# A two-layer decoder trunk: six of eight attention-branch gates by seven products, and values and gates kept by head pairs

## The chip, the cores and the metric

The kernel runs on one core of one Trainium2 chip, in one launch. The metric is the device time of that launch in microseconds (us), as the median of several runs. A profile is one more execution, recorded by the hardware profiler, with a time of its own. Engines are named as the profile names them: PE is the matrix engine (TensorE) and PEld its loading of weights, DVE is VectorE, ACT is ScalarE, POOL is GpSimd, SP is SyncE, which here only issues transfers.

## The reference

All data is float32: 512 tokens (S), width 1024 (D), two layers. Each layer is a feed-forward part, a mixer, and a second feed-forward part, each with a norm before and after. The change is in the mixer alone:

```python
for l in range(DEPTH):                                  # DEPTH = 2
    ...
    h = rms_norm(x, gn[2])
    proj = h @ w_in[l]
    hq, hf, hi, hg, aq, ak, av, gate_a, gate_b = jnp.split(proj, IN_SPLITS, axis=-1)
    y_hg = hgrn2_mixer(hq, hf, hi, hg, lb_all[l], hgrn_head_gain[l]) @ w_branch_hgrn[l]
    y_at = swa_sink_attention(aq, ak, av, attn_sinks[l]) @ w_branch_attn[l]
    mixed = jax.nn.sigmoid(gate_a) * y_hg + jax.nn.sigmoid(gate_b) * y_at
    x = x + rms_norm(mixed @ w_out[l], gn[3])
    ...
```

`hgrn2_mixer` is a gated linear recurrence over four heads of 128, from which come the values `hi` and a gate `hg` on the output; `swa_sink_attention` is attention over a window of 128 tokens, eight heads of 64, in four blocks of 128 queries, with one more logit per head (the sink) in the denominator. `gate_a` and `gate_b`, 1024 wide each, gate the two branches that are added.

## The kernel before

**Numbers in halves.** Each float32 operand is split into a high part that PE takes in its faster format, and the low part that is left (`split`: ACT writes the high part, DVE subtracts). A product of two tiles of 128 x 128 by 512 columns is three matmuls, high by high, low by high, high by low (line 116). Line 126 is a transpose through PE.

**Weights** come from memory through `Stream`, `ws` in the code, in units of 128 x 1024 in the order of their use: SP issues the load (`w<-wall`), ACT casts the high part (line 359), DVE subtracts the low one (line 363); for some kinds of unit the low part is instead ACT's negated copy (line 355), to which a transfer issued by POOL adds the weights (line 358). The stream splits at least three units ahead of PE, has four buffers for raw units and six for each part of split ones.

**Seven products for eight.** `sevenths` makes two output tiles at once from seven products of 256 columns (an algorithm of Strassen's kind), each four blocks deep, where two plain tiles take eight blocks of 512 columns each. Its weights are four units of a pair: the first is plain, the second and third are sums of the pair's two raw units, which DVE makes (lines 341 to 345) in buffers of the tag `tt`, the fourth is a plain half. Behind the products DVE puts the two tiles together (lines 1063 to 1070). A matmul of 144 columns, `lead`, goes ahead of a pair. The moving operands are also sums, of quarters of the mixer's input, made once per layer (`pre.sums`, four calls) and kept.

**The tag `tt` has two buffers**, and the recurrence draws from it as well, once per head and level:

```python
self.t13 = sb.tile([P, D], F32, tag="tt", name=nm("tt"), bufs=2)                 # Stream, a pair's second unit
self.t = t = sb.tile([P, D], F32, tag="tt", name=nm("tt"), bufs=2)               # and its third
self.mv = mv = sb.tile([P, 2 * TT, 96], F32, tag="tt", name=nm("mv"), bufs=2)    # recurrence, before a level
```

**What sets the order.** PE runs in the order in which the code issues its work. Side work, which is the recurrence and the attention, is written as coroutines (`order.spawn`), each of which names a time in `WAIT` until its next step is due; between two blocks of weights the code runs the steps that are due by its own clock of PE's work. On the other engines a scheduler sets the order when the kernel is built. An engine then works through its list in that order.

**The mixer** runs in this order: the projections of recurrence heads 0 and 1 (`quad`, by seven products), keys, queries and values of the attention, four token tiles of recurrence values (`vs`), four of output gates (`gs`), the projections of heads 2 and 3, eight tiles of the attention branch, each a gate by a plain product (`project`) and four blocks of the branch's own weights (`branch`, `LATE = 8` of them), four pairs of tiles of the recurrence branch with their gates by seven products (`branches(recurred)`), and the output product (`down`). The four attention blocks (`attend`: scores on PE, the mask and the maximum on DVE, lines 1357 to 1368, the exponentials on ACT, line 1374, transposes of the shares on PE, copies of those on ACT, line 1396, and their product with the values) run between the projections of values, gates and heads 2 and 3; the attention branch needs all four (`attended`). The recurrence of heads 2 and 3 (per level `mv` on ACT and DVE, line 1188, products on PE, then `place`, line 1164, `queries` and `keys`, lines 1172 to 1179, on DVE) runs between the eight tiles of the attention branch; the recurrence branch needs it (`recurred`). Tanh and gating of `gs` are lines 1428 and 1429, those of a branch tile line 1444 on DVE.

PSUM has eight banks: five of the tag `acc`, in which the projections collect, and three of the tag `aux`, for everything else. Names in the profile such as `s`, `acc`, `aux`, `tt`, `whi`, `wlo` are these tags and tiles.

Of the kernel before, what the change touches and what calls it, by code (L numbers as in the profile page):

```python
# [7 lines left out]
F32 = mybir.dt.float32  # L8
F32R = mybir.dt.float32r
# [24 lines left out]
    head=2600.0, level=5000.0, last=3400.0, chunks=2600.0, states=2600.0, norm=2370.0, gate=8000.0,  # L34
    values=1200.0, scores=2000.0, exp=9000.0, shares=6000.0, turn=1900.0, turned=3000.0, rest=1200.0, lent=4200.0, apart=4000.0, block=2000.0, pair=4000.0, att0=1260.0, att1=12300.0,
)
W32, WS, AHEAD, TAIL, FIRST, EARLY, LATE = 4, 6, 3, 4, 7, 4, 8
TURN = 0
SEVEN = 16
ASIDE = 16  # L40
# [6 lines left out]
def trunk(ctx: ExitStack, tc: tile.TileContext, xin, wall, gains, lbT, hgain, sinks, c_dist, c_mask, c_ident, out):  # L47
# [16 lines left out]
    def big(dt=F32, shape=None):  # L64
        return sb.tile(shape or [P, S], dt, tag="s", name=nm("s"), bufs=SLOTS)
# [4 lines left out]
    def acc():  # L70
        return ps.tile([P, S], F32, tag="acc", name=nm("acc"), bufs=5)

    def aux():
        return ps.tile([P, S], F32, tag="aux", name=nm("aux"), bufs=3)
# [350 lines left out]
    def cut(pair, c):  # L425
        return pair[0][:, c], pair[1][:, c]
# [73 lines left out]
    def pair_split(v, how=split):  # L500
        return how(v, to=(big(F32R, [P, 2, S // 2]), big(F32R, [P, 2, S // 2])))
# [77 lines left out]
    class Pre(Quarters):  # L579


        def __init__(self, l, n):
            self.l, self.n = l, n
            self.h = []
            self.have = [0, 0]
            self.rb = None
            self.xn = {}
            self.x56, self.x37 = [], []

        def sums(self):  # L590
            k = len(self.x56)
            a = []
            for hi, lo in (self.h[k], self.h[k + 4]):
                f = big()
                nc.vector.tensor_tensor(f, hi.bitcast(F32), lo.bitcast(F32), op=ALU.add)
                a.append([f[:, c] for c in HALF])
            for x, v in zip((self.x56, self.x37), quarter_sums(a[0][0], a[1][0], a[0][1], a[1][1])):
                x.append(pair_split(v))

        def raw(self, half, i):  # L600
            return [cut(self.h[k + 4 * i], HALF[half]) for k in range(4)]
# [431 lines left out]

        mm(o[:, :n], st, mv[:, :n], True, True)

    def sevenths(pre, between=lambda: None, first=True):

        def product(o, it, c, n):  # L1040
            x = pre.operand(n)
            for k in range(4):
                wmm(o, ws.block(it, c + k), x[k], k == 0, k == 3)

        p1, p26, p57, p43 = acc()[:, :H2], acc(), acc(), aux()
        s, v = big()[:, :H2], big(F32, [P, 2, H2])
        w = ws.whole()
        if first:
            lead(p1, w.hi[:, :P], pre.operand(1)[0][0], LEAD)
        product(p1, w, 0, 1)  # L1050
        ws.hold(nc.scalar.copy(s, p1))
        product(p26[:, :H2], w, 4, 2)
        between()
        w = ws.whole()
        product(p57[:, :H2], w, 0, 5)
        product(p57[:, H2:], w, 4, 7)
        c = ws.whole()
        product(p26[:, H2:], c, 0, 6)
        ws.product()
        m = sb.tile([P, 4, H2], F32, tag="m", name=nm("m"), bufs=1)  # L1060
        pairs = [p.rearrange("p (i t) -> p i t", i=2) for p in (p26, p57, p43)]

        ws.hold(nc.vector.tensor_tensor(m[:, 0:4:2, :], pairs[0], s.unsqueeze(1).to_broadcast([P, 2, H2]), op=ALU.add))

        ws.hold(nc.vector.tensor_tensor(v, pairs[1], m[:, 2:3, :].to_broadcast([P, 2, H2]), op=ALU.add))
        product(p43[:, :H2], c, 4, 4)
        product(p43[:, H2:], ws.whole(), 4, 3)

        ws.hold(nc.vector.tensor_tensor(m[:, 3, :], p57[:, :H2], v[:, 1, :], op=ALU.add))
        ws.hold(nc.vector.tensor_tensor(m[:, 1:3, :], pairs[2], v[:, ::-1, :], op=ALU.add))  # L1070
        return m
# [178 lines left out]
    def chunk_states(hs, vs, i):  # L1250

        pu = [aux() for _ in hs]
        for n, (h, p) in enumerate(zip(hs, pu)):
            d = slice((i + n) * P, (i + n + 1) * P)
            for c in range(TT - 1):
                mm(p[:, c * P : (c + 1) * P], h.kt[:, c * P : (c + 1) * P], vs[c][:, d], True, True)
        for h, p in zip(hs, pu):
            h.st = big()
            nc.scalar.copy(h.st[:, :P], p[:, :P])
        for c in (1, 2):  # L1260
            for h, p in zip(hs, pu):
                o, u = (h.st[:, (c - x) * P : (c - x + 1) * P] for x in (0, 1))
                nc.vector.scalar_tensor_tensor(o, u, h.prod[:, c : c + 1], p[:, c * P : (c + 1) * P], op0=ALU.mult, op1=ALU.add)
        yield WAIT["states"]

    def mixer(l, pre, nxt):
        vs, gs = [], []
        oa = [None] * H

        def head(ph, pq, i):  # L1270
            f, k, q, th = big(), big(), big(), big()
# [8 lines left out]
        def outputs(i, h):  # L1280
            po = aux()
            for t in range(TT):
                c = slice(t * P, (t + 1) * P)
                mm(po[:, c], h.sd[:, t, :], vs[t][:, i * P : (i + 1) * P], True, t == 0)
                if t:
                    mm(po[:, c], h.qa[:, c], h.st[:, (t - 1) * P : t * P], False, True)
            pov = po.rearrange("p (t d) -> p t d", t=TT)
            sq = big()
            nc.scalar.activation(out=sq, in_=po, func=AF.Square)
            ss = small([P, TT], "ss")  # L1290
            nc.vector.tensor_reduce(ss, sq.rearrange("p (t d) -> p t d", t=TT), axis=AX.X, op=ALU.add)
            nc.scalar.activation(out=ss, in_=ss, func=AF.Sqrt, bias=eps_t, scale=1.0 / P)
            nc.vector.reciprocal(ss, ss)
            o = big(F32, [P, TT, P])
            nc.vector.tensor_tensor(o, pov, ss.unsqueeze(2).to_broadcast([P, TT, P]), op=ALU.mult)
            yield WAIT["norm"]
            while len(gs) < TT:
                yield 500.0
            for t in range(TT):
                nc.vector.tensor_tensor(o[:, t, :], o[:, t, :], gs[t][:, i * P : (i + 1) * P], op=ALU.mult)  # L1300
            yield WAIT["gate"]
            pt = aux()
            for t in range(TT):
                transpose(pt[:, t * P : (t + 1) * P], o[:, t, :])
            oa[i] = split(pt)

        def run(i, heads):
            yield WAIT["head"]
            box = []
            yield from recurrence_scores(heads, box)  # L1310
            if len(vs) < TT:
                while len(vs) < TT:
                    yield 500.0
                yield WAIT["lent"]
            yield from chunk_states(box, vs, i)
            for n in range(2):
                order.spawn(outputs(i + n, box[n]), n * WAIT["apart"])
# [101 lines left out]
        order.spawn(attention((1, 3)), WAIT["att1"])  # L1419


        for i, p in enumerate(project_tok(pre)):
            v = big()
            (nc.vector.tensor_copy if i % 2 else nc.scalar.copy)(v, p)
            vs.append(v)
        for p in project_tok(pre):
            g = big()
            nc.scalar.activation(out=g, in_=p, func=AF.Tanh, scale=0.5)
            nc.vector.scalar_tensor_tensor(g, g, 1.0, p, op0=ALU.add, op1=ALU.mult)
            gv = g.rearrange("p (i d) -> p i d", i=H)  # L1430
            nc.vector.tensor_tensor(gv, gv, hgh[:, l : l + 1, :].to_broadcast([P, H, P]), op=ALU.mult)
            gs.append(g)
        order.spawn(run(2, [head(project(pre), project(pre), i) for i in range(2, H)]))


        def branch(get):
            p = project(pre)
            g = big()
            nc.scalar.activation(out=g, in_=p, func=AF.Tanh, scale=0.5)
            p = acc()  # L1440
            src = get()
            for k in range(4):
                wmm(p, ws.next(), src[k], k == 0, k == 3)
            nc.vector.scalar_tensor_tensor(g, g, 1.0, p, op0=ALU.add, op1=ALU.mult)
            return g

        def branches(get):

            v = sevenths(pre)
            src = get()  # L1450
            for i in range(2):
                g = big(F32, [P, 2, H2])
                nc.scalar.activation(out=g, in_=v[:, 2 * i : 2 * i + 2, :], func=AF.Tanh, scale=-0.5 if i else 0.5)
                p = acc()
                for k in range(4):
                    wmm(p, ws.next(), src[k], k == 0, k == 3)
                g = g.rearrange("p i t -> p (i t)")
                nc.vector.scalar_tensor_tensor(g, g, 1.0, p, op0=ALU.add, op1=ALU.mult)
                yield g
# [8 lines left out]

        part = []
        for m in range(LATE):  # L1470
            if m >= LATE - 4:
                pre.sums()
            part.append(branch(attended))
        part += [g for m in range(LATE, KT, 2) for g in branches(attended)]
        mixed = []
        for m in range(0, KT, 2):
            for g in branches(recurred):
# [174 lines left out]
```

## Time and profile before

| what | before |
|---|---|
| median of three runs | 2024.1 us (2024.02, 2024.10, 2025.45) |
| the profiled execution's own time | 2024.79 us |
| its span | 2023.0 us |
| TensorE's granted clock, mean | 1.00 |
| PE busy | 2016.2 us, 13553 matmuls |
| DVE busy | 1624.3 us, 2894 instructions |
| ACT busy | 1265.2 us, 2213 instructions |
| POOL busy | 268.3 us, 318 instructions |
| read from memory | 213.43 MB |

The span runs from the first to the last recorded instruction. A row of a group reads: line, engine, operation, output tile <- inputs, shape, count | busy us, mean ns of one | idle us of the engine ahead of them, and what ended most of it. A row of waits reads: who waited, with what, <- for whom: sum in us, how often, the longest. A row of the timeline reads: start, length, engine, line, operation, shape, and how many instructions in a row it stands for. A row of windows reads: the stretch in us from the span's start, then busy times.

### The profile page before, as it was taken

The numbers are of one execution on the slowest core, as the hardware profiler recorded it, in microseconds if no ns is written. First come the engines' busy times: TensorE is split into PE (matmuls) and PEld (weight loads), VectorE is DVE, ScalarE is ACT, GpSimd is POOL, SyncE is SP. The second block draws the span as 40 slices with busy tenths as digits, with TensorE's granted clock in tenths as the row PEclk, the third lists the DMA queues.
The fourth block names the chain that finished last, engine by engine and source line by source line (L and its number), as shares of the span: only waits on it lengthen the run. The fifth ranks groups of instructions, "written<-read, shape, count | busy, mean of one in ns | idle before, by whom it ended". The sixth has DMA issues, their size and how long they took to land.

```text
span 2023.0 us, 36425 instructions
## 1 busy us (share of the span) xinstructions
PE 2016.2 (100%) x13553; PEld 1809.1 (89%) x13553; DVE 1624.3 (80%) x2894; ACT 1265.2 (63%) x2213; POOL 268.3 (13%) x318
## 2 busy tenths in 40 slices
PE   9999999999999999999999999999999999999998
PEld 8899988877898999998899998898778989999987
DVE  5888899767786788888998888977686858888888
ACT  7566687447364566658766666864554646666684
POOL 0111140000000011113211111400000100111140
PEclk9999999999999999999999999999999999999999
DMA  8688798311246368879768888872122554788794
GB/s 257 159 193 198 177 203 244 109 63 64 83 104 208 112 158 190 193 189 208 202 170 196 196 190 203 189 223 86 61 74 63 151 182 123 170 193 200 175 202 122
DMA packets 166801, 328.07 MB, mean 162 GB/s; under 512 B 19072, under 2 KB 85088, under 8 KB 166624
## 3 DMA queue, kind: packets, MB, share of 16 engines
q1 hardware_dynamic: 122416, 228.16, 34.1%
q0 software_dynamic: 44064, 97.54, 28.5%
q8 instruction: 106, 1.74, 0.3%
q14 instruction: 71, 0.58, 0.1%
q10 hardware_dynamic: 144, 0.05, 0.0%
HBM read 213.43 MB, written 14.73 MB: 113 GB/s over the span
## 4 chain that ended last, share of the span: by engine, by line
PE 93%; DVE 3%; ACT 1%; DMA 1%; issue 1%; SPq 0%; DVEq 0%; ACTq 0%
PE acc L116 71%; PE aux L116 20%; PE aux L126 2%; DVE wlo L296 1%; DVE s L264 1%; DMA w<-wall 1%; PE acc L126 0%; ACT whi L288 0%; DVE s L968 0%; SPq L244 0%; ACT s L442 0%; ACT s L443 0%; DVE wlo L363 0%; DVE s L863 0%; DVE s L433 0%
## 5 line engine op out<-in xcount | busy, mean ns | idle before, releaser
L116 PE MATMUL acc<-s,whi 128*128 128x256 f32 (+1 forms) x4998 | 1018.9, 303 | 0.0
L116 PEld LDWEIGHTS acc<-s,whi 128*128 128x128 f32 x4998 | 791.5, 188 | 46.6 <-issue 3.2
L116 PE MATMUL acc<-s,wlo 128*128 128x256 f32 (+1 forms) x2488 | 752.5, 302 | 0.1
L116 PEld LDWEIGHTS acc<-s,wlo 128*128 128x128 f32 x2488 | 467.9, 188 | 23.3 <-DVE wlo L363 0.4
L116 PE MATMUL acc<-whi,s 128*128 128x512 f32 x1360 | 441.5, 393 | 0.0
L359 ACT CAST whi<-w 128x1024 fp32r<-128x1024 f32 (+1 forms) x310 | 286.1, 926 | 195.0 <-PE acc L116 124.5
L358 POOL DMA_DIRECT2D wlo<-w x178 | 154.6, 869 | 1200.2 <-ACT wlo L355 715.0
L116 PEld LDWEIGHTS acc<-whi,s 128*128 128x128 f32 x1360 | 255.3, 188 | 57.1 <-issue 3.2
L116 PE MATMUL acc<-wlo,s 128*128 128x512 f32 x680 | 265.5, 390 | 0.2 <-DVE wlo L296 0.2
L355 ACT ACTIVATE wlo<-w 128x1024 fp32r<-128x1024 f32 (+1 forms) x178 | 154.6, 869 | 137.1 <-PE aux L116 98.2
L116 PE MATMUL aux<-s,whi 128*128 128x256 f32 (+1 forms) x1296 | 226.9, 278 | 0.0
L359 ACT CAST whi<-tt 128x1024 fp32r<-128x1024 f32 x160 | 168.4, 1053 | 83.2 <-DVE tt L341 43.0
L363 DVE TENSOR_TENSOR wlo<-w,whi 128x1024 fp32r<-128x1024 f32 (+1 forms) x132 | 157.4, 1205 | 78.3 <-ACT whi L359 78.1
L363 DVE TENSOR_TENSOR wlo<-tt,whi 128x1024 fp32r<-128x1024 f32 x160 | 195.4, 1221 | 9.9 <-ACT whi L359 7.3
L116 PEld LDWEIGHTS aux<-s,whi 128*128 128x128 f32 x1296 | 195.8, 188 | 1.1 <-issue 0.5
L116 PE MATMUL aux<-s,wlo 128*128 128x256 f32 (+1 forms) x648 | 179.8, 277 | 0.0
L116 PEld LDWEIGHTS acc<-wlo,s 128*128 128x128 f32 x680 | 127.8, 188 | 27.0 <-DVE wlo L296 2.1
L116 PE MATMUL aux<-whi,s 128*128 128x512 f32 x432 | 143.7, 390 | 0.0
L444 POOL DMA_DIRECT2D s<-s x128 | 111.1, 967 | 223.5 <-ACT s L432 104.7
L116 PEld LDWEIGHTS aux<-s,wlo 128*128 128x128 f32 x648 | 121.6, 188 | 0.4
L296 DVE TENSOR_TENSOR wlo<-s,whi 128x512 fp32r<-128x512 f32 x160 | 102.7, 686 | 9.9 <-ACT whi L288 9.9
L1070 DVE TENSOR_TENSOR m<-aux,s 128x512 f32<-128x512 f32 x80 | 55.2, 690 | 52.0 <-PE aux L116 51.5
(184 smaller groups left out, 2485.1 us busy)
## 6 DMA issues: line engine op xcount, KB each, us to landing
w<-wall SPq DMA_DIRECT2D x267, 512.0 KB, 3.9
wlo<-w POOLq DMA_DIRECT2D x98, 512.0 KB, 5.4
w<-wall SPq DMA_DIRECT2D x224, 128.0 KB, 3.5
wlo<-w POOLq DMA_DIRECT2D x80, 256.0 KB, 4.2
s<-wall SPq DMA_DIRECT2D x128, 128.0 KB, 4.2
s<-s POOLq DMA_DIRECT2D x64, 256.0 KB, 4.6
x_d<-s SPq DMA_DIRECT2D x48, 256.0 KB, 4.7
s<-x_d SPq DMA_DIRECT2D x48, 256.0 KB, 5.1
```

The costliest lines, as they stand in the source:

```text
L116: nc.tensor.matmul(o, lhsT, rhs, start=start, stop=stop)
L126: nc.tensor.transpose(o, src, ident)
L264: pin(nc.vector.tensor_tensor(o[c], x[c], y[c], op=op))
L296: pin(nc.vector.tensor_tensor(it.lo[:, h[c]], w[c], it.hi[:, h[c]].bitcast(F32), op=ALU.subtract))
L355: i = nc.scalar.mul(it.lo[:, c], w[:, c], -1.0)
L358: nc.gpsimd.dma_start(it.lo[:, c].bitcast(F32), w[:, c], accum_op=ALU.add)
L359: i = nc.scalar.copy(it.hi[:, c], w[:, c])
L363: self.hold(nc.vector.tensor_tensor(it.lo[:, c], w[:, c], it.hi[:, c].bitcast(F32), op=ALU.subtract))
L444: nc.gpsimd.dma_start(lo.bitcast(F32), src, accum_op=ALU.add)
L1070: ws.hold(nc.vector.tensor_tensor(m[:, 1:3, :], pairs[2], v[:, ::-1, :], op=ALU.add))
```

## The change

- `LATE` is 2 instead of 8: two of the eight attention-branch tiles stay plain, the other six are three pairs by `sevenths`. Those collect their last two products in a bank of `acc` instead of `aux`. The stream announces three plain units per plain branch tile, and seven pairs (`gates`) instead of four.
- The operand sums are made earlier: four calls of `pre.within` during the projections of heads 2 and 3 (behind the second, third and fourth) and the first plain branch tile, instead of four calls of `pre.sums` ahead of the last four plain branch tiles. `pre.within` keeps the sum of the third operand unsplit, and `pre.third` splits it later, inside the first `sevenths`, into memory of the input that is no longer needed.
- `vs` and `gs` are stored as tiles of [128, 2 token tiles, 256], one set per pair of heads: two copies of 256 columns on ACT or DVE per token tile where there was one of 512, two products with the head gain of 256 columns each for one of 512, and the gating of a head's output is two products of 256 elements per row for four of 128.
- The outputs of heads 0 and 1 are kept as one plain tile each (one ACT copy) and split into high and low part ahead of the last pair of the attention branch.

Per layer six gate tiles drop 144 matmuls of 512 columns; three pairs take 252 of 256 columns and three of 144. In the whole kernel PE has 222 instructions more, DVE 52, ACT 46, POOL 12, SP 12. Lines of the file shift: 116 becomes 117, 126 becomes 127, 341 to 345 become 342 to 346, 359 and 363 become 360 and 364, 1063 to 1070 become 1085 to 1092, 1164 becomes 1186, 1172 to 1179 become 1194 to 1201, 1188 becomes 1210, 1369 and 1374 become 1395 and 1400, 1396 becomes 1422, 1428 becomes 1456.

```diff
-W32, WS, AHEAD, TAIL, FIRST, EARLY, LATE = 4, 6, 3, 4, 7, 4, 8
+W32, WS, AHEAD, TAIL, FIRST, EARLY, LATE = 4, 6, 3, 4, 7, 4, 2
+SUMS = ("h1", "h2", "h3", 0)
...
+        def within(self):
+            s, t = self.quarters()
+            self.x56.append(pair_split(s))
+            x = big(F32R, [P, 2, S // 2])
+            self.x7.append(split(t[:, 1, :], to=(x[:, 0, :], x[:, 1, :])))
+            self.t3.append(t[:, 0, :])
+
+        def third(self):
+            while self.t3:
+                self.x3.append(split(self.t3.pop(0), to=cut(self.h[len(self.x3)], HALF[1])))
...
-    def sevenths(pre, between=lambda: None, first=True):
+    def sevenths(pre, between=lambda: None, first=True, get=aux):
...
-        p1, p26, p57, p43 = acc()[:, :H2], acc(), acc(), aux()
+        p1, p26, p57, p43 = acc()[:, :H2], acc(), acc(), get()
...
-            for t in range(TT):
-                nc.vector.tensor_tensor(o[:, t, :], o[:, t, :], gs[t][:, i * P : (i + 1) * P], op=ALU.mult)
+            for t in range(0, TT, 2):
+                g = gs[i // 2][t // 2][:, :, i % 2 * P : (i % 2 + 1) * P]
+                nc.vector.tensor_tensor(o[:, t : t + 2, :], o[:, t : t + 2, :], g, op=ALU.mult)
...
-            oa[i] = split(pt)
+            if i < 2:
+                oa[i] = big()
+                nc.scalar.copy(oa[i], pt)
+            else:
+                oa[i] = split(pt)
...
+        for t, p in enumerate(project_tok(pre)):
+            for n in range(2):
+                if not t % 2:
+                    vs[n].append(big(F32, [P, 2, S // 2]))
+                (nc.vector.tensor_copy if t % 2 else nc.scalar.copy)(vs[n][-1][:, t % 2, :], p[:, HALF[n]])
...
+            for n in range(2):
+                if not t % 2:
+                    gs[n].append(big(F32, [P, 2, S // 2]))
+                nc.vector.tensor_tensor(
+                    gs[n][-1][:, t % 2, :].rearrange("p (i d) -> p i d", i=2), g[:, HALF[n]].rearrange("p (i d) -> p i d", i=2),
+                    hgh[:, l : l + 1, :].to_broadcast([P, 2, P]), op=ALU.mult,
+                )
...
+        def project_sums(n):
+            o = project(pre)
+            if n in SUMS:
+                pre.within()
+            return o
...
-        def branches(get):
-
-            v = sevenths(pre)
+        def branches(get, bank=aux):
+
+            v = sevenths(pre, pre.third, get=bank)
...
         for m in range(LATE):
-            if m >= LATE - 4:
-                pre.sums()
             part.append(branch(attended))
-        part += [g for m in range(LATE, KT, 2) for g in branches(attended)]
+        for m in range(LATE, KT, 2):
+            if m == KT - 2:
+                oa[:2] = [split(o) for o in oa[:2]]
+            part += branches(attended, acc)
```

The prediction speaks of two places where the order on an engine changes. The first is ACT in layer 0 around the last tile of the output gates (tanh, line 1428) and the last attention block's copies from `aux` (line 1396). Before, ACT runs:

```order
L1428 ACTIVATE s_5440<-acc_5085 128x512
L1428 ACTIVATE s_5444<-acc_5086 128x512
L1428 ACTIVATE s_5448<-acc_5087 128x512
L1428 ACTIVATE s_5452<-acc_5088 128x512
L1396 COPY s_5502<-aux_5492 128x512
L1396 COPY s_5503<-aux_5493 128x512
L1396 COPY s_5525<-aux_5515 128x512
L1396 COPY s_5526<-aux_5516 128x512
L359 CAST whi_5641<-w_966_5335 128x1024
L432 CAST s_5553<-aux_5548 128x512
L1374 ACTIVATE s_5380,den_5477<-s_5380,neg_5472 128x256
```

The copies follow the tanh rows at once, and the other attention block's exponentials (line 1374) come behind them. In the changed kernel ACT runs, at the same place:

```order
L1456 ACTIVATE s_5444<-acc_5089 128x512
L1456 ACTIVATE s_5451<-acc_5090 128x512
L1456 ACTIVATE s_5456<-acc_5091 128x512
L1395 ACTIVATE es_5482<-es_5482 128x8
L1400 ACTIVATE s_5384,den_5485<-s_5384,neg_5480 128x256 x2
L1400 ACTIVATE s_5388,den_5485<-s_5388,neg_5480 128x256 x2
L1456 ACTIVATE s_5463<-acc_5092 128x512
L1400 ACTIVATE s_5430,den_5485<-s_5430,neg_5480 128x256 x2
L1400 ACTIVATE s_5434,den_5485<-s_5434,neg_5480 128x256 x2
L1422 COPY s_5510<-aux_5500 128x512
L1422 COPY s_5511<-aux_5501 128x512
L1422 COPY s_5533<-aux_5523 128x512
```

The eight exponentials, `es` and the last tanh now stand ahead of the copies. On PE the transposes of that block in the changed kernel, with the semaphores that they wait for:

```order
L127 MATMUL aux_5523<-ident,s_5191 128x128 [waits DVE_49]
L127 MATMUL aux_5523<-ident,s_5191 128x128
L127 MATMUL aux_5523<-ident,s_5245 128x128 x2
L127 MATMUL aux_5524<-ident,s_5195 128x128 [waits Activation_49]
L127 MATMUL aux_5524<-ident,s_5195 128x128
L127 MATMUL aux_5524<-ident,s_5249 128x128 x2
L117 MATMUL acc_5468<-s_4129,whi_5128 128x512
```

They stand at the same place among the products as before; the second four wait for ACT, since their bank is the one that the first of the copies reads.

The second place is DVE in layer 0 in the recurrence of heads 2 and 3, from the end of its second level's work to the third level's `mv`. Before:

```order
L1172 TENSOR_TENSOR s_5745<-s_5745,s_5749 128x16x16
L1164 COPY_PREDICATED s_5752<-mask,aux_5931 128x4x4x8
L1188 TENSOR_TENSOR mv_5989<-s_5745,s_5749 128x8x32
L1164 COPY_PREDICATED s_5752<-mask,aux_5931 128x4x4x8
L1172 TENSOR_TENSOR s_5750<-s_5750,s_5754 128x16x16
L1172 TENSOR_TENSOR s_5745<-s_5745,s_5749 128x8x32
L1188 TENSOR_TENSOR mv_5994<-s_5750,s_5754 128x8x32
L363 TENSOR_TENSOR wlo_6084<-w_1055_5866,whi_6083 128x1024
```

Both heads' `mv` follow the recurrence's own rows. In the changed kernel:

```order
L342 TENSOR_TENSOR tt_6106<-w_1091_5985 128x512
L344 TENSOR_TENSOR tt_6109<-tt_6106,w_1091_5985 128x512
L1085 TENSOR_TENSOR m_6123<-acc_5993,s_5996 128x2x256
L346 TENSOR_TENSOR tt_6109<-tt_6109,w_1026_5668 128x512
L364 TENSOR_TENSOR wlo_6105<-tt_6106,whi_6104 128x1024
L1087 TENSOR_TENSOR s_5997<-acc_5994,m_6123 128x512
L364 TENSOR_TENSOR wlo_6152<-tt_6109,whi_6151 128x1024
L1194 TENSOR_TENSOR s_5801<-s_5801,s_5805 128x16x16
L1091 TENSOR_TENSOR m_6123<-acc_5994,s_5997 128x256
L1210 TENSOR_TENSOR mv_6129<-s_5801,s_5805 128x8x32
```

The sums of a pair's weights (`tt`), their splits into `wlo` and the sums behind the products (`m`) now stand between the recurrence's rows, and `mv` follows when both `tt` have been split.

More of the change, by code (lines that the diff above doesn't have):

```diff
@@ L588, in __init__, with quarters @@
             self.x56, self.x37 = [], []
-        def sums(self):
+            self.x3, self.x7, self.t3 = [], [], []
+        def quarters(self):
             k = len(self.x56)
@@ L596, in sums, with operand @@
                 a.append([f[:, c] for c in HALF])
-            for x, v in zip((self.x56, self.x37), quarter_sums(a[0][0], a[1][0], a[0][1], a[1][1])):
+            return quarter_sums(a[0][0], a[1][0], a[0][1], a[1][1])
+        def sums(self):
+            for x, v in zip((self.x56, self.x37), self.quarters()):
                 x.append(pair_split(v))
+        def within(self):
[7 more added lines that the diff above has]
+                self.x3.append(split(self.t3.pop(0), to=cut(self.h[len(self.x3)], HALF[1])))
+        def operand(self, n):
+            if n in (3, 7) and self.x7:
+                return self.x3 if n == 3 else self.x7
+            return super().operand(n)
         def raw(self, half, i):
@@ L1253, in chunk_states @@
         for n, (h, p) in enumerate(zip(hs, pu)):
-            d = slice((i + n) * P, (i + n + 1) * P)
             for c in range(TT - 1):
-                mm(p[:, c * P : (c + 1) * P], h.kt[:, c * P : (c + 1) * P], vs[c][:, d], True, True)
+                mm(p[:, c * P : (c + 1) * P], h.kt[:, c * P : (c + 1) * P], vs[i // 2][c // 2][:, c % 2, n * P : (n + 1) * P], True, True)
         for h, p in zip(hs, pu):
@@ L1266, in mixer @@
     def mixer(l, pre, nxt):
-        vs, gs = [], []
-        oa = [None] * H
+        vs, gs = [[], []], [[], []]
+        oa, done, gated_o = [None] * H, [], []
         def head(ph, pq, i):
@@ L1283, in outputs @@
                 c = slice(t * P, (t + 1) * P)
-                mm(po[:, c], h.sd[:, t, :], vs[t][:, i * P : (i + 1) * P], True, t == 0)
+                mm(po[:, c], h.sd[:, t, :], vs[i // 2][t // 2][:, t % 2, i % 2 * P : (i % 2 + 1) * P], True, t == 0)
                 if t:
@@ L1296, in outputs @@
             yield WAIT["norm"]
-            while len(gs) < TT:
+            while not gated_o:
                 yield 500.0
-            for t in range(TT):
-                nc.vector.tensor_tensor(o[:, t, :], o[:, t, :], gs[t][:, i * P : (i + 1) * P], op=ALU.mult)
+            for t in range(0, TT, 2):
+                g = gs[i // 2][t // 2][:, :, i % 2 * P : (i % 2 + 1) * P]
+                nc.vector.tensor_tensor(o[:, t : t + 2, :], o[:, t : t + 2, :], g, op=ALU.mult)
             yield WAIT["gate"]
@@ L1310, in run @@
             yield from recurrence_scores(heads, box)
-            if len(vs) < TT:
-                while len(vs) < TT:
+            if not done:
+                while not done:
                     yield 500.0
@@ L1419, in mixer @@
         order.spawn(attention((1, 3)), WAIT["att1"])
[L1422 to L1426, printed above, removed]
+        for t, p in enumerate(project_tok(pre)):
[3 more added lines that the diff above has]
+                (nc.vector.tensor_copy if t % 2 else nc.scalar.copy)(vs[n][-1][:, t % 2, :], p[:, HALF[n]])
+        done.append(True)
+        for t, p in enumerate(project_tok(pre)):
             g = big()
@@ L1429, in mixer @@
             nc.vector.scalar_tensor_tensor(g, g, 1.0, p, op0=ALU.add, op1=ALU.mult)
[L1430 to L1433, printed above, removed]
+            for n in range(2):
[5 more added lines that the diff above has]
+                )
+        gated_o.append(True)
+        def project_sums(n):
[3 more added lines that the diff above has]
+            return o
+        order.spawn(run(2, [head(project_sums(f"h{2 * i}"), project_sums(f"h{2 * i + 1}"), 2 + i) for i in range(2)]))
         def branch(get):
-            p = project(pre)
+            p = project_sums(len(part))
             g = big()
```

## Prediction

> **What bounds the kernel now.** I read the page's first part and its chain, then who waited for whom on TensorE, then the stretch that the change touches in layer 0.
>
> ```profile
> PE 2016.2 (100%) x13553; PEld 1809.1 (89%) x13553; DVE 1624.3 (80%) x2894; ACT 1265.2 (63%) x2213; POOL 268.3 (13%) x318
> PE 93%; DVE 3%; ACT 1%; DMA 1%; issue 1%; SPq 0%; DVEq 0%; ACTq 0%
> ```
> ```profile
> PE aux L116 <- DVE eps_t L139: 1.1, 1, 1.1
> PE acc L126 <- DVE s L863: 1.0, 2, 0.5
> PE acc L116 <- DVE wlo L296: 0.2, 1, 0.2
> ```
> ```profile
> 471.00:576.00 105.00, 105.00 (x620) 84.90 (x619) 78.59 (x187) 56.51 (x106) 1.47 (x3) 1.00 0.22 71
> ```
>
> TensorE is busy for 2016.2 of the 2023.0 us; the second fence holds all its waits, 2.3 us in sum and none of them in the mixer. So a column fewer on TensorE is time won, and any wait that is new there is time lost in full. The last row is the stretch from the gate projection to the end of the attention branches (columns: PE, weight loads, DVE, ACT and POOL busy, granted clock, DMA share, GB/s). TensorE has no gap in its 105 us, DVE works for 78.6, ACT for 56.5.
>
> **What TensorE saves.** Three rows give the step from one matmul to the next, in stretches of one shape.
>
> ```profile
> 643.00:677.00 34.00, 34.00 (x152) 1.00 0.43 147
> 745.00:855.00 110.00, 110.00 (x973) 1.00 0.82 196
> 523.25:524.73 1.48, 1.48 (x34) 1.00 0.27 55
> ```
>
> The first holds products of 512 columns: without the two at the edges 34.00/150 = 0.2267 us. The second holds 256 columns: 110.00/971 = 0.1133 us. The third is one level of the recurrence, 1.48 us for two heads. Per layer, six tiles' gates were 6 x 8 x 3 = 144 products of 512 columns and become 3 x 7 x 4 x 3 = 252 of 256; three leading products of 144 columns come with them, by their columns 0.064 us each. That is 32.6 us off and 28.6 + 0.2 us on: 3.9 us less per layer, 7.8 in the kernel.
>
> **What DVE gets.** Of a pair of tiles it drops two splits of 1024 columns and takes on four sums of 512 for the weights, two splits of 1024, and three sums of 512 and one of 256 behind the products. Its steps, from the rows of the next part: 1.14 us for 1024, 0.60 for 512, 0.33 for 256. So a pair adds 7 x 0.60 + 0.33 = 4.5 us, three pairs 13.6, and the late splits of the third operand (4 x 0.33) 1.3. The operand sums themselves were made before too, later. DVE then has 93.5 us of work in some 101 us of TensorE's, 92% where it had 75%. A queue that full delays what stands in it. The order shows two places per layer, the same rows in both layers, where TensorE waits for such a row.
>
> **First place: the last attention block's transposes.** Rows of ACT, of DVE and of TensorE, as they run before the change:
>
> ```profile
> 472.90 1.28 ACT L1428 ACT_TABLE_LOAD   x1
> 474.19 2.07 ACT L1428 ACTIVATE s<-acc 128x512 f32<-128x512 f32 x4
> 476.12 1.11 ACT L1396 COPY s<-aux 128x512 f32<-128x512 f32 x2
> 484.24 0.49 ACT L1374 ACTIVATE s<-s,neg 128x256 f32<-128x256 f32 x1
> 484.64 0.19 ACT L1374 ACTIVATION_READ_ACCUMULATOR s<-s,neg 128x1 f32 x1
> 484.73 0.49 ACT L1374 ACTIVATE s<-s,neg 128x256 f32<-128x256 f32 x1
> ```
> ```profile
> 471.66 1.07 DVE L1357 SCALAR_TENSOR_TENSOR s<-dist,aux 128x256 f32<-128x256 f32 x3
> 473.57 1.22 DVE L363 TENSOR_TENSOR wlo<-w,whi 128x1024 fp32r<-128x1024 f32 x1
> 474.71 0.68 DVE L1362 TENSOR_REDUCE mxs<-s 128x2 f32<-128x512 f32 x1
> 475.31 1.28 DVE L1429 SCALAR_TENSOR_TENSOR s<-s,acc 128x512 f32<-128x512 f32 x2
> 482.93 0.17 DVE L1366 TENSOR_SCALAR neg<-mxs 128x8 f32<-128x8 f32 x1
> 483.00 0.17 DVE L1368 TENSOR_TENSOR es<-sink,mxs 128x8 f32<-128x8 f32 x1
> ```
> ```profile
> 477.32 1.03 PE L126 MATMUL aux<-ident,s 128*128 128x128 f32 x8
> 478.11 0.71 PE L116 MATMUL acc<-s,whi 128*128 128x512 f32 x2
> ```
>
> A start column beside the next gives the steps: 474.71 - 473.57 = 1.14, (1.28 - 0.68 of one) = 0.60, three of 256 in 1.07 with 0.41 of one at the end = 0.33, the small ones 0.07. On ACT an exponential with its accumulator takes 484.73 - 484.24 = 0.49, a tanh (2.07 - 0.6)/3 = 0.5. The eight transposes begin at 477.32 and step by 0.1, so the second four, which need the bank that the first copy (476.12 to 476.7) empties, begin at 477.7. Before, they find it free by 1.0 us. In the new order eight exponentials and the last tanh stand ahead of that copy, and the first of them needs `neg` and `es`. DVE reaches these after its reduce: 475.31, one gate of 512 (0.60), the maximum with the sink (0.1), two halves of 256 (0.67), `neg` and `es` with the tail of the last (0.3), so 477.0. ACT: `es` 0.1, eight exponentials 3.9, a tanh 0.5, the copy 0.6, done at 482.1, and TensorE goes on at 482.2 instead of 477.7. That is 4.5 us per layer, 9.0 in all. The bounds: by ACT's rows alone, from the third tanh at 475.8, 3.3 us; with the second copy awaited too, 5.0.
>
> [...]
>
> **Second place: the recurrence of heads 2 and 3.** The tag `tt` has two buffers. They hold the recurrence's `mv` and, for a pair's second and third item, the sums of weights. Before, no such sums were made while `mv` was in use; now each level's `mv` waits until both sums are split, and the sums wait until TensorE has read `mv`. Before, from the end of level one on TensorE to the third level's `mv`:
>
> ```profile
> 511.82:528.48 16.66, 14.22 (x46) 1.00 0.25 81
> ```
> ```profile
> 480.10 1.71 DVE L1300 TENSOR_TENSOR s<-s,s 128x128 f32<-128x128 f32 x8
> 525.06 0.28 DVE L1164 COPY_PREDICATED s<-mask,aux 128x128 f32<-128x128 int32 x1
> 525.26 0.42 DVE L1177 TENSOR_TENSOR s<-s,s 128x256 f32<-128x256 f32 x1
> ```
>
> 46 DVE instructions, 14.2 us busy. In the new order 64 stand there, from the first row of `tt_5835` to `mv_6134`: 11 of 512 (6.6), 30 of 256 (10.0), 5 of 1024 (5.7), 14 of 128 at 0.2, as 525.26 - 525.06 and (1.71 - 0.29)/7 show (2.8), and 4 shorter ones (0.5), in sum 25.6 us, and with 0.3 for the matmul's and the last row's tails 25.9. TensorE has between the same two points 45 products of 512, 84 of 256, a lead, and one and a half levels: 10.2 + 9.5 + 0.1 + 2.2 = 22.0 us. So it waits 3.9 us there, 7.8 in both layers, in two or three pieces. The pause of the first place does not help, since the first of the 64 is itself released by TensorE. The cast of a sum on ACT has this row:
>
> ```profile
> L359 ACT CAST whi<-tt 128x1024 fp32r<-128x1024 f32 x160 | 168.4, 1053 | 83.2 <-DVE tt L341 43.0
> ```
>
> Bounds: 0 if part of the rows is overtaken, and if each of the four casts that free a `tt` (1.05 us) comes to stand in the chain, 4.2 more per layer.
>
> **What costs nothing.** Values, gates and the products with them in halves: eight of 256 for four of 512 and eight of 256 for sixteen of 128 on DVE, 8 x 0.33 - 4 x 0.60 + 8 x 0.33 - 16 x 0.20 = -0.3 us, two more copies on ACT and DVE each, 0.2 us, two copies of heads 0 and 1 with their splits later: under the 26 us in which DVE and the 48 in which ACT idles; what stands ahead of `neg` is counted above. The queues: SP issues 24 halves for 12 whole units, POOL 12 more accumulations.
>
> ```profile
> w<-wall SPq DMA_DIRECT2D x267, 512.0 KB, 3.9
> wlo<-w POOLq DMA_DIRECT2D x98, 512.0 KB, 5.4
> ```
>
> They land in 3.9 and 5.4 us; the stream splits at least three items ahead, 8.2 us of products, at a DMA share of 0.22 and POOL 1.5 us busy. Uncovered, an accumulation would show its 5.4 us once per pair. If a bank of `acc` comes free late, the next pair waits for one sum, 0.6 us.
>
> **The sum.** -7.8 + 9.0 + 7.8 = +9.0 us. The profiled execution took 2024.8 us (span 2023.0, 1.8 around it), 0.7 over the median of 2024.1. From the median: 2033.
>
> **Rivals.** *Only the first wait remains*: the pause lets DVE run ahead by 4.5 us, more than the 3.9 that it lacks. For it speaks that DVE idles 26 us of the stretch, against it that the 64 rows begin with one that TensorE releases. -7.8 + 9.0 = +1.2: 2025, no change. It decides from 3.9 us of the 25.9 done early. *No wait remains*: the sum of columns alone, 2016, faster. That needs the copy ready 4.5 us sooner, which the order forbids if ACT works in order. [...] *The casts join the chain*: 4.2 us more per layer, 2041.
>
> **How the numbers follow.** Forecast 0.46 (its own range 2028.5 to 2037), only the first wait 0.17, none 0.10, the clock 0.14, the casts 0.13. 0.2% of 2024 is 4 us, about what a measurement here can tell from no change. So faster 0.10, same 0.17, slower 0.73. The range leaves out the case without waits and the upper end of the last one: 2022 to 2042.
>
> **What would show it.** Of the first place: the page's waits name ACT L1422 for TensorE, about 4.5 us twice, at about 478 and 1477 us. Of the second: waits for DVE L1210 or ACT L1206/L1208 (`mv`), some 4 us per layer. TensorE's instructions rise by 222, its busy time falls by about 8 us. DVE in the stretch stands above 90%. [...] Wrong I would be if these rows are not waited for, or if waits of the same size stand elsewhere.

## The result, and the profile after

The changed kernel takes 2042.25 us (median of four runs, 2041.54 to 2043.39) against 2024.18 us before: the ratio is 1.0088, with a 95% interval of 1.0071 to 1.0106. That is 18.1 us slower, where 9 were forecast, and just above the range. The profiled execution has a span of 2041.6 us where the one before had 2023.0.

From the page of the changed kernel, the busy times:

```profile
PE 2019.1 (99%) x13775; PEld 1821.4 (89%) x13775; DVE 1652.6 (81%) x2946; ACT 1286.2 (63%) x2259; POOL 278.6 (14%) x330
```

TensorE has the 222 instructions more that were forecast, but its busy time rose by 2.9 us instead of falling by 7.8. Whom it waited for, in the same execution:

```profile
PE aux L127 <- ACT s L1422: 8.5, 2, 4.3
PE aux L117 <- DVE mv L1210: 4.6, 4, 2.1
PE aux L117 <- DVE s L1201: 1.9, 2, 0.9
PE aux L117 <- DVE eps_t L140: 1.1, 1, 1.1
PE acc L127 <- DVE s L885: 1.0, 2, 0.5
PE aux L117 <- ACT mv L1208: 0.5, 2, 0.3
PE acc L117 <- DVE wlo L297: 0.3, 1, 0.3
```

The rows for `eps_t` and L885 were there before, and the last one with 0.2. The other four are new, 15.5 us in sum: the first place with 8.5 and the recurrence of heads 2 and 3 with 7.0. The forecast had 9.0 and 7.8 at the same lines. The waits explain 15.5 of the 18.6 us; that the busy time rose is something else. TensorE's rows around the first pause in layer 0 (start, length):

```profile
477.61 0.60 PE L127 MATMUL aux<-ident,s 128*128 128x128 f32 x4
482.42 1.12 PE L127 MATMUL aux<-ident,s 128*128 128x128 f32 x4 [4.22 <-ACT s L1422]
484.19 0.63 PE L117 MATMUL acc<-s,wlo 128*128 128x512 f32 x1
484.62 1.05 PE L117 MATMUL acc<-s,whi 128*128 128x512 f32 x2
...
488.03 0.59 PE L117 MATMUL acc<-s,wlo 128*128 128x512 f32 x1
488.46 0.60 PE L127 MATMUL aux<-ident,s 128*128 128x128 f32 x4
488.81 0.71 PE L117 MATMUL acc<-s,whi 128*128 128x512 f32 x2
```

From 484.19 to 484.62 one product of 512 columns takes 0.43 us, where 0.227 was the step before: nearly double. That ends with the row at 488.03. The granted clock (the column behind PE's busy time and count) says the same, here in stretches of 5 us:

```profile
480.00:485.00 5.00, 2.58 (x8) 0.66 0.00 0
485.00:490.00 5.00, 5.00 (x18) 0.66 0.30 105
545.00:550.00 5.00, 3.89 (x36) 0.65 0.63 145
550.00:555.00 5.00, 5.00 (x20) 0.67 0.35 103
1490.00:1495.00 5.00, 2.98 (x9) 0.70 0.00 0
1550.00:1555.00 5.00, 2.39 (x23) 1.00 0.61 156
```

The clock fell behind three of the four places: behind both first pauses (482 and 1492 us) and, in layer 0 alone, behind the pauses for `mv` (547 us). In the granted clock, which is 0.50 throughout them, the three spells run from 481.6 to 488.4, from 546.5 to 553.3 and from 1492.0 to 1495.4 us, and TensorE goes on at 482.4, 547.0 and 1492.0. Summed over the products, they cost 3.0, 3.1 and 1.7 us more than the steps of before: 7.8 us.

### The profile page after: what moved, and what is told of

Read it like the earlier page. It is cut to its first block, busy times and chain, and to the rows that moved or that the text cites. A ratio compares the mean times of both kernels' runs of the same rounds, so it can differ in the third digit from the quotient of the medians.

```text
span 2041.6 us, 37048 instructions
## 1 busy us (share of the span) xinstructions
PE 2019.1 (99%) x13775; PEld 1821.4 (89%) x13775; DVE 1652.6 (81%) x2946; ACT 1286.2 (63%) x2259; POOL 278.6 (14%) x330
## 4 chain that ended last, share of the span: by engine, by line
PE 46%; DVE 5%; ACT 1%; issue 1%; DMA 1%; SPq 0%; DVEq 0%; ACTq 0%
PE acc L117 34%; PE aux L117 10%; DVE wlo L297 1%; DVE s L265 1%; PE aux L127 1%; DVE wlo L364 1%; DVE s L990 0%; DMA w<-wall 0%; PE acc L127 0%; ACT s L443 0%; DVE s L434 0%; DVE s L885 0%; ACT s L1400 0%; ACT whi L289 0%; DVE s L859 0%
## 5 line engine op out<-in xcount | busy, mean ns | idle before, releaser
L117 PEld LDWEIGHTS acc<-s,whi 128*128 128x128 f32 x5148 | 810.4, 188 | 40.7 <-issue 3.5
L117 PE MATMUL acc<-s,wlo 128*128 128x256 f32 (+1 forms) x2560 | 763.9, 298 | 0.0
L117 PEld LDWEIGHTS acc<-s,wlo 128*128 128x128 f32 x2560 | 482.9, 189 | 19.7
L359 POOL DMA_DIRECT2D wlo<-w x190 | 165.0, 868 | 1478.3 <-ACT wlo L356 869.8
L356 ACT ACTIVATE wlo<-w 128x1024 fp32r<-128x1024 f32 (+1 forms) x190 | 164.8, 867 | 138.5 <-PE aux L117 98.0
L360 ACT CAST whi<-tt 128x1024 fp32r<-128x1024 f32 x172 | 180.8, 1052 | 106.7 <-DVE tt L342 60.0
L364 DVE TENSOR_TENSOR wlo<-tt,whi 128x1024 fp32r<-128x1024 f32 x172 | 209.9, 1221 | 14.3 <-ACT whi L360 9.3
L364 DVE TENSOR_TENSOR wlo<-w,whi 128x1024 fp32r<-128x1024 f32 (+1 forms) x120 | 142.8, 1203 | 70.3 <-ACT whi L360 68.8
L297 DVE TENSOR_TENSOR wlo<-s,whi 128x512 fp32r<-128x512 f32 x160 | 102.6, 683 | 9.9 <-ACT whi L289 9.9
L434 DVE TENSOR_TENSOR s<-s,s 128x512 fp32r<-128x512 f32 (+1 forms) x152 | 83.6, 580 | 19.4 <-ACT s L433 19.0
```

The lines of the kernel that those rows point to most:

```text
L117: nc.tensor.matmul(o, lhsT, rhs, start=start, stop=stop)
L297: pin(nc.vector.tensor_tensor(it.lo[:, h[c]], w[c], it.hi[:, h[c]].bitcast(F32), op=ALU.subtract))
L356: i = nc.scalar.mul(it.lo[:, c], w[:, c], -1.0)
L359: nc.gpsimd.dma_start(it.lo[:, c].bitcast(F32), w[:, c], accum_op=ALU.add)
L360: i = nc.scalar.copy(it.hi[:, c], w[:, c])
L364: self.hold(nc.vector.tensor_tensor(it.lo[:, c], w[:, c], it.hi[:, c].bitcast(F32), op=ALU.subtract))
```

## The experiments

Each run's ratio is against runs of the kernel before on the same chip.

**The storage alone.** The kernel before with values, gates and the outputs of heads 0 and 1 stored as in the change, all eight attention-branch tiles plain:

```diff
-W32, WS, AHEAD, TAIL, FIRST, EARLY, LATE = 4, 6, 3, 4, 7, 4, 2
-SUMS = ("h1", "h2", "h3", 0)
+W32, WS, AHEAD, TAIL, FIRST, EARLY, LATE = 4, 6, 3, 4, 7, 4, 8
+SUMS = ()
...
+            if m >= LATE - 4:
+                pre.sums()
...
+        oa[:2] = [split(o) for o in oa[:2]] if LATE == KT else oa[:2]
```

> The kernel before with only the storage of the change: values and gates by head pairs, heads 0 and 1 kept plain and split later; eight plain attention-branch tiles, operand sums where they were. In its order the eight exponentials stand ahead of the last attention block's copies, as in the changed kernel. Theory (the storage alone makes the first wait, 4.2 us per layer, and the wait alone halves the clock for 3 to 6 us behind it): TensorE waits 8.5 us for ACT's copies (L1422), loses 0.2 us per restart and 3 to 6 us to the clock in sum; 2036 to 2039 us. Rival (the wait came from the seven products or the earlier operand sums): no such wait, 2024 us, as before.

Measured: 2037.8 us, ratio 1.0062 (1.0048 to 1.0076), 12.9 us slower. Its one new wait is this:

```profile
PE aux L127 <- ACT s L1422: 8.4, 2, 4.2
```

So the storage, with all eight tiles of the attention branch plain, makes the whole first place. Eight exponentials stand ahead of two copies on ACT, and 13 of the 18 us follow.

**Gates in whole tiles.** The changed kernel with only the gates as before:

```diff
...
-                nc.vector.tensor_tensor(
-                    gs[n][-1][:, t % 2, :].rearrange("p (i d) -> p i d", i=2), g[:, HALF[n]].rearrange("p (i d) -> p i d", i=2),
-                    hgh[:, l : l + 1, :].to_broadcast([P, 2, P]), op=ALU.mult,
-                )
+            gv = g.rearrange("p (i d) -> p i d", i=H)
+            nc.vector.tensor_tensor(gv, gv, hgh[:, l : l + 1, :].to_broadcast([P, H, P]), op=ALU.mult)
+            gs[0].append(g)
```

> The changed kernel, with the recurrence's output gates alone stored as before, as whole tiles of four heads (one DVE product of 512 for two of 256 per token tile, four gatings of 128 for two of 256 per head). In its order ACT's copies stand ahead of the exponentials again. Theory: the first wait goes (8.5 us), with its two restarts (0.4) and its share of the slow clock (4.7); the second place's waits stay at 7.0 us, with their slow spell where it falls: 2026 to 2031 us. Rival 1 (the pause of the first place gave DVE time that the second place then lacks): the second place's waits grow by up to 8.5 us, 2033 to 2038. Rival 2 (another instruction holds the copies): 2042, as changed.

Measured: 2032.5 us, ratio 1.0040 (1.0026 to 1.0053); its four executions lie far apart, from 2030.6 to 2036.0 us, and the profiled one is the slowest. ACT's row of copies now follows the tanh at once, as before the change, and the wait of 4.2 us is gone:

```profile
474.38 2.07 ACT L1455 ACTIVATE s<-acc 128x512 f32<-128x512 f32 x4
476.30 1.11 ACT L1421 COPY s<-aux 128x512 f32<-128x512 f32 x2
```

It is 1.5 us above the range expected. A wait appears that the pause had hidden (the block after it: its copies stood behind an operand sum's casts), and the waits for `mv` grew a little:

```profile
PE aux L117 <- DVE mv L1210: 5.8, 6, 2.0
PE aux L127 <- ACT s L1421: 2.2, 2, 1.1
```

So an edit on DVE, one product less per token tile and two gatings more per head, put ACT's order right: the scheduler sets it, and a small edit elsewhere turned it over. Which of the two decided is not shown.

**A tag of its own for `mv`.** The changed kernel with

```diff
-            self.mv = mv = sb.tile([P, 2 * TT, 96], F32, tag="tt", name=nm("mv"), bufs=2)
+            self.mv = mv = sb.tile([P, 2 * TT, 96], F32, tag="mv", name=nm("mv"), bufs=2)
...
-SLOTS = 61
+SLOTS = 58
```

> The changed kernel, with the recurrence's mv in a tag of its own with two buffers; the tag s has 58 slots instead of 61 to make room. Theory 1 (mv and the weights' sums wait for each other's buffers): the second place's waits for mv (5.1 us, and most of the 1.9 for s of L1201) go, with their restarts (1.3) and the slow spell of layer 0 (3.1): 2031 to 2034 us. Theory 2 (DVE has too much to do there, whatever the buffers; its queue has no idle time from 528 to 547 us): only what stands between the two mv now goes, some 1.2 us per layer, 2038 to 2042 us. If 58 slots are too few, waits for other buffers appear and the time rises above 2042.

Measured: 2040.9 us, ratio 1.0080 (1.0066 to 1.0094). By its time alone the second theory would win. The waits say otherwise:

```profile
PE aux L127 <- ACT s L1422: 8.5, 2, 4.3
PE acc L117 <- DVE wlo L297: 3.1, 8, 0.8
PE aux L117 <- ACT mv L1208: 2.3, 2, 1.3
PE aux L117 <- ACT s L1073: 0.6, 2, 0.3
```

In the second place 2.9 of the 7.0 us are left. In layer 0 the clock does not fall there: behind a wait of 0.98 us TensorE steps by 0.23 us. So with buffers of its own for `mv` 4.1 us of the wait are gone. Part of the gain went to waits for `wlo` of L297, 3.1 us where the changed kernel had 0.3, all in stages outside the mixer. The three slots fewer are the likely cause, but no run has them alone, and what else they cost was not taken apart.

**The first pause filled.** Matmuls of no use in the pause, with the order on ACT and DVE unchanged:

```diff
                 for e in range(2):
+                    if e and n == 2 and b == 1:
+                        d = acc()
+                        for _ in range(36):
+                            nc.tensor.matmul(d[:, :256], kS[0][:, :P], kS[0][:, :256], start=True, stop=True)
```

> The changed kernel, with 36 matmuls of 256 columns, whose result is overwritten unread, put on TensorE into the first place's pause, ahead of the transposes that wait for ACT's copy. The order on ACT and DVE is the same as in the changed kernel. 36 x 0.113 = 4.1 us of work in a pause of 4.2 us. Theory (the pause itself costs 8.5 us, and the clock halved by it 3.0 and 1.7 us more): the pause is full, the copy comes when it came, and the slow spells at 482 and 1492 us are gone: 2042.3 - 4.7 - 0.3 = 2037 us. Rival (the slow matmuls behind the pause have another cause, such as contention with ACT or DVE): 2042, as changed, with the spells where they were.

Measured: 2037.9 us, ratio 1.0068 (1.0056 to 1.0081). TensorE's rows at the same place:

```profile
479.15 4.55 PE L1420 MATMUL acc<-s 128*128 128x256 f32 x36
483.61 0.66 PE L127 MATMUL aux<-ident,s 128*128 128x128 f32 x4
484.02 0.71 PE L117 MATMUL acc<-s,whi 128*128 128x512 f32 x2
484.57 0.40 PE L117 MATMUL acc<-s,wlo 128*128 128x512 f32 x1
```

The matmuls behind it step by 0.23 us, with the same work on the other engines beside them. The granted clock there is 1.00 in both layers, where it was 0.50 behind the empty pauses. So here the idle time itself lowers the clock: 18.1 us over the kernel before became 13.0 (the five executions reach from 2036.4 to 2042.2 us). The pause's own length is not won back, since the matmuls of no use stand in its place.

**Half of the pause filled**, 18 instead of 36 matmuls:

> The changed kernel with 18 instead of 36 matmuls in the first place's pause: 2.0 us of work, and 2.2 us of pause left. [...]

Measured: 2043.1 us, ratio 1.0090 (1.0074 to 1.0105), no faster than the changed kernel. At the first place the pauses left are 2.13 and 2.06 us long, and behind them the clock stayed at 1.00 in both layers. But in this execution it fell behind the second place in both:

```profile
480.00:485.00 5.00, 2.87 (x24) 1.00 0.00 1
545.00:550.00 5.00, 4.05 (x24) 0.51 0.48 134
1490.00:1495.00 5.00, 4.12 (x22) 1.00 0.00 0
1552.00:1557.00 5.00, 4.32 (x23) 0.50 0.39 118
```

The mean granted clock is 0.996 in all four executions, so each lost about as much; where the other three lost it is not on record, and how pauses of 2.1 us fare on the average stays open.

**One operand sum moved, and the recurrence asked for later.** Three steps from the run with whole gates: the sum of h2 moved to h0, and then on top of it the products of each level of heads 2 and 3 due 2.5 or 5 us later.

```diff
-SUMS = ("h1", "h2", "h3", 0)
+SUMS = ("h0", "h1", "h3", 0)
...
-            yield WAIT["pair"]
+            yield WAIT["pair"] + late      # 0, or 2500 or 5000 for heads 2 and 3
```

> As the run with whole gates, and one operand sum moved from the projection h2 to h0 (SUMS h0, h1, h3, 0), so that on ACT the last attention block's copies stand ahead of that sum's casts, not behind them. Theory: of the run with whole gates (2032.5 us) the waits for these copies (2 x 1.1 us and 2 x 0.2 for the restarts) go: 2029 to 2031 us, TensorE's waits in the second place stay at 8.2 us, each level asked for too early. Rival (the copies' wait only moves into the second place, since DVE and ACT have no time to spare): 2032 us.

Measured: 2030.1 us, ratio 1.0026 (1.0017 to 1.0035); the copies' wait is gone and 7.4 us in the second place stay. Its ten executions lie in three groups, at 2027.7 to 2028.1, at 2029.7 to 2030.8 and at 2032.0 to 2033.9 us; the profiled one is of the first group, and its mean granted clock is 1.000.

> The same, and in the recurrence of heads 2 and 3 each level's products come 2.5 us later on TensorE's own count (the due time behind mv is 6.5 instead of 4.0 us). Theory (mv is late since DVE has more rows between two levels than TensorE has products; the recurrence's end has some 10 us to spare before the recurrence branch needs it): the waits for mv (second level 1.0 us, third 2.7 us per layer, and 2.8 us of slow clock per layer behind them) go by two thirds or more: 2018 to 2022 us. Rival 1 (the scheduler moves mv back by as much, since the two buffers of tt are given to the weights' sums first): waits stay, 2029 to 2031. Rival 2 (the later recurrence is waited for at its end): waits at the recurrence branch, over 2024.

Measured: 2019.8 us, ratio 0.9975 (0.9966 to 0.9984), faster than both kernels. All waits of TensorE:

```profile
PE aux L117 <- DVE eps_t L140: 1.1, 1, 1.1
PE acc L127 <- DVE s L885: 1.0, 2, 0.5
PE acc L117 <- DVE wlo L297: 0.3, 1, 0.3
```

Nothing is left that was not there before the change but 0.1 us, though DVE works 101 of 115 us in the stretch:

```profile
470.00:585.00 115.00, 115.00 (x823) 100.03 (x820) 101.08 (x229) 70.08 (x134) 8.35 (x11) 1.00 0.38 100
```

> The same with 5 us per level. In the order the last head's transposes then stand at the very product that needs them. Theory: no wait for mv is left, and the end of the recurrence is waited for instead, up to 3 us per layer: 2016 to 2024 us; without that wait the columns alone would give 2024.2 - 8 + 0.3 = 2016.5. Rival (as in the run with 2.5 us): waits for mv stay, 2029 to 2031.

Measured: 2021.6 us, ratio 0.9984 (0.9975 to 0.9993). Also no wait for `mv`, and small ones at the end of the recurrence instead:

```profile
PE acc L117 <- DVE s L434: 0.8, 2, 0.4
PE aux L117 <- ACT s L1268: 0.5, 2, 0.3
```

**The second place alone.** The changed kernel with nothing but the 2.5 us:

> The changed kernel with only the recurrence of heads 2 and 3 asked for later, 2.5 us per level; values, gates and operand sums as in the change. Theory (the two places are independent, and the second one is a matter of when TensorE asks): the waits for mv (7.0 us) go with their eight restarts (1.3) and the slow spells behind them (3 us in the profiled execution), the first place stays with 8.5 us of waits and its slow clock: 2029 to 2032 us. Rival (the first place's pause is what lets DVE catch up, or the second place is bound by DVE's work however late it is asked for): waits for mv of 3 us or more stay, 2034 or more.

Measured: 2033.1 us, ratio 1.0040 (1.0026 to 1.0054), one us above the range expected. TensorE's waits at the two places:

```profile
PE aux L127 <- ACT s L1422: 8.4, 2, 4.2
```

No wait for `mv` is left, and the first place stands as it was: the two are independent. The parts also nearly add up: 12.9 us for the first place (the storage alone), 9.7 for the second (ratio 1.0088 against 1.0040) and -5.1 for the columns make 17.5 of the 18.1 us. The second place was not short of DVE over the whole stretch; it was short at the moment at which TensorE asked.

## Why the prediction failed

| term | forecast us | measured us | by |
|---|---|---|---|
| fewer columns | -7.8 | -5.1 | the run at 2019.8 us, which has no new wait |
| first place, waits | +9.0 | +8.5 | waits after |
| second place, waits | +7.8 | +7.0 | waits after |
| restarts behind ten pauses | 0 | +1.7 | about 0.17 us of each beyond the wait |
| slow clock | 0 | +7.8 | steps in three spells |

The measured column adds up to 19.9, the profiles differ by 18.6; the columns' term comes from a kernel with its own order, and the difference of 1.3 us is left.

- **The bound and the places were right.** A new wait of TensorE is time lost, and both places, their lines and their sizes came as worked out. In the first one ACT's `es` started at 477.28 us (worked out: 477.0) and TensorE went on at 482.4 (482.2), while the whole changed kernel ran some 0.3 us later there than the one before:

```profile
477.28 0.21 ACT L1395 ACTIVATE es<-es 128x8 f32<-128x8 f32 x1 [1.22 <-DVE es L1394]
481.80 1.52 ACT L1422 COPY s<-aux 128x512 f32<-128x512 f32 x3
```

- **The step that failed is the clock.** The sum has no term for it, though the chances gave it 0.14. No row of before shows a slow clock to price it from: the granted clock is 1.00 throughout the mixer, and TensorE's longest wait in the whole kernel is 1.1 us. After the change it was 0.50 for 6.83, 6.83 and 3.41 us, and cost 7.8 us. The second place took part without one long pause: 1.76 and 0.94 us of idle time with 0.9 us of small products between were enough in layer 0. And the loss doesn't go by the pause's length: 4.22 and 4.26 us of it cost 3.0 and 1.7 us, since the clock stayed down for 6.83 us behind the one and for 3.41 us behind the other. With 7.8 us for the clock the sum would have been 2041.
- **The restarts were left out.** The sum puts them at nothing without a reason, though the profile before has a wait to read one from: at 2017.47 us there are 0.80 us from one matmul to the next across a wait of 0.53, 0.16 more than the wait and a step. After the change, from one matmul to the next across the wait of 4.26 us at 1492 us there are 4.54 us, 0.17 more than the wait and a step; the other nine pauses give 0.16 to 0.21.
- **The columns were overrated.** They gave 5.1 instead of 7.8 us. The same products of 256 columns of the first pair take 7.90 us in layer 0 and 7.60 in layer 1, 4% apart:

```profile
533.28:541.18 7.90, 7.90 (x70) 1.00 0.79 201
1541.68:1549.28 7.60, 7.60 (x70) 1.00 0.83 209
```

  A step of 0.118 us instead of 0.1133 for all 504 products would be 2.3 us; that is an upper bound, since part of them step by 0.1133 to 0.114. Why some stretches step so, at a full granted clock, was not found.
- **The reason given for the second place was half of it.** The shared tag carried some 4.1 of 7.0 us, as far as the run with a tag of its own shows, which also had three slots fewer. One sign did not come: DVE was to stand above 90% in the stretch, but worked for 96.55 of 119.70 us from 471.3 us on (81%), and for 101.08 of 115.00 (88%) in the run at 2019.8 us. Its work in the whole kernel grew nearly as worked out, by 28.3 us against 2 x 14.9. That TensorE could simply ask later the prediction did not look at: with three levels of 2.5 us more the recurrence's end is not yet waited for, with three of 5 us by 0.65 us per layer. The casts did not join the chain.

## What to carry to other kernels

When a change reorders a queue, find the waits, and then add what an idle matrix engine costs beyond the wait: here some 0.17 us for each restart, and a clock of 0.50 for 3.4 or 6.8 us behind three of the four places (next section). Look at each part of an edit by itself: a change of storage that seemed free cost 13 us by turning ACT's order over, and hid that the products themselves saved 5. And where work waits on a due time with slack behind it, move the due time before adding buffers.

## What the runs showed of the hardware

The slow spells in the changed kernel end where a step of 512 columns falls from 0.43 to 0.23 us:

```profile
488.03 0.59 PE L117 MATMUL acc<-s,wlo 128*128 128x512 f32 x1
552.48 1.01 PE L117 MATMUL acc<-s,whi 128*128 128x512 f32 x2
553.32 0.40 PE L117 MATMUL acc<-s,wlo 128*128 128x512 f32 x1
1495.06 0.55 PE L117 MATMUL acc<-s,wlo 128*128 128x512 f32 x1
1495.45 0.62 PE L117 MATMUL acc<-s,whi 128*128 128x512 f32 x2
```

In the trace's record of the granted clock they last 6.827, 6.827 and 3.413 us and end at 488.45, 553.30 and 1495.38 us, 64.85 and 1006.93 us apart: 19 and 295 times the shortest spell. No run shows what sets these times, nor why the pause of 4.22 us had a spell of 6.83 us behind it and the one of 4.26 us only 3.41.

How much TensorE stood still does not alone decide whether the clock falls. Of the 3.4 us up to each fall TensorE was busy for 0 us (from 478.20 us on), 1.19 us (543.10) and 0 us (1488.60). In layer 1 the waits for `mv` were longer, 2.05 and 0.94 us, and left it busy for 0.91 of the 3.41 us from 1552.00 us on, but the clock stayed at 1.00. What decides is not shown.

The mean granted clock of the ten executions with one operand sum moved, which fall into groups some 2 to 3 us apart, goes with these groups: 0.999 to 1.000 in the fastest, 0.998 to 0.999 in the middle one and 0.996 to 0.998 in the slowest. Only one of them has a trace, so where the others lost the clock is open.
